# One of five products of the attention scores on half the rows of the array, for two query blocks side by side

## The chip, the cores and the metric

The kernel runs on one core of a Trainium2 chip. The metric is the time of one execution on the device in microseconds (us). Five engines work side by side on a core: TensorE (PE in the profile; its weight loads have a row of their own, PEld), VectorE (DVE), ScalarE (ACT), GpSimd (POOL) and SyncE (SP), which here only issues DMAs. TensorE multiplies a stationary operand, held in an array of 128 rows and 128 columns, with a moving operand that streams through it, and accumulates in the banks of PSUM. The rows of the array are the dimension that is summed over.

## The reference

One layer of a hybrid decoder over 1024 positions of width 1024: layer norm, one input projection, a state-space branch (S5) and an attention branch (MLA) beside each other, an output projection, a gated embedding, a closing layer norm. All is in 32-bit floats. What the change touches are the scores of the attention, with 4 heads and blocks of 128 queries:

```python
q = concatenate([q[..., :QK_NOPE], rotary(q[..., QK_NOPE:], cos, sin)], axis=-1)   # 128 + 64
k = concatenate([k_nope, broadcast(rotary(kr, cos, sin), heads)], axis=-1)
s = einsum('bqhd,bkhd->bhqk', qb, k) * scale
s = where(key_pos <= q_pos, s, -inf)
pr = softmax(s, axis=-1)
out = einsum('bhqk,bkhd->bqhd', pr, v)
```

The rotary part of a query has 64 numbers, that of a key too, and all heads share the keys' rotary part.

## The kernel before

**Split products.** TensorE takes its operands rounded to a shorter form. To stay near full precision, the kernel splits each operand into hi (the rounded value) and lo (the rest), and makes three products (`mm3`, line 518): hi by hi, hi by lo, lo by hi. Line 441, to which the profile puts every instruction, is only where the recorded instructions are issued; groups are told apart by their tiles.

**The scores** (`scores`, line 914) are made per head h and block qb of 128 queries, against the first n = (qb+1)*128 keys, in pieces c:e of at most 512 columns. A piece takes five products into one PSUM tile `s`. Three are an `mm3` of the part without rotation (tiles qnh, qnl, kh, kl). Two are of the rotary part. Since that has only 64 numbers, its tiles hold two copies one above the other: the 128 rows of `qr` are hi over lo of q, those of `krh` are twice the keys' hi, those of `krl` twice the keys' lo. So the product of `qr` with `krh` sums q hi and q lo by k hi in one go, and the product of `qr` with `krl` sums q hi and q lo by k lo:

```python
mm3(o, qn[h][0][:, q], qn[h][1][:, q], kh[:, c:e], kl[:, c:e], True, False)
mm(o, qr[h][:, q], L["kr"][0][:, c:e], False, False)
mm(o, qr[h][:, q], L["kr"][1][:, c:e], False, True)
```

The pieces are 128 columns (qb = 0), 256, 384, 512 (qb = 1 to 3), 320 and 320 (qb = 4), 512 and 256, 512 and 384, 512 and 512 (qb = 5 to 7). A score of up to 512 columns takes one of four small PSUM buffers (`PB`), a longer one takes one of two large ones (`PA`), which S5's tiles `w` and `y` use too. Then the softmax: VectorE adds the mask and takes the maximum (tile `p`, from `s`), ScalarE the exponential, and the result is scaled by the reciprocal of the sum.

**`q_rope`** (line 867) makes rotary q and splits it into the two halves of tile `qd`; `q_rope_t` transposes `qd` to `qr`.

**Items.** The attention goes through 16 items (h, j) in the order of the list `ATTEND`; an item is the two query blocks 2j and 2j+1. The loop at line 1522 writes, for each i: the scores of item i, the transposes of the probabilities of item i-1 (`probs_t`, tiles pt, pth, ptl), the product with the values of item i-2 (`pv`, tile o), the last projection of item i-3 (`uv_out`, tile uv), and late pieces of S5 and of its gate (`glu`).

**The order of the work.** The code doesn't issue instructions; it records them in a `Plan`. `Plan.issue` (line 308) then lays them out with prices of its own for each operation (for a product 0.012 us and 0.425 ns a column, at least 0.11 us where the weights change) and takes on each engine the ready instruction with the lowest number, once its buffers are free. So the order on each engine comes from the order of the recording, from the shifts in `AHEAD` and `SHIFT`, and from the prices. Whatever changes a price changes the order of all that comes after.

Of the kernel before, what the change touches and what calls it, by code (L numbers as in the profile page):

```python
# [17 lines left out]

# [1 line left out]

# [14 lines left out]
P = 128  # L35
# [84 lines left out]
class Plan:  # L120
# [74 lines left out]
    def record(self, ways, args=()):  # L195
        _, method, kw = ways[0]
        isap = lambda x: hasattr(x, "tensor") and hasattr(x, "ap")
        outs = [kw[k] for k in ("out", "accum_out") if isap(kw.get(k))]
        rest = [v for k, v in kw.items() if isap(v) and k not in ("out", "accum_out")]
        pos = [a for a in args if isap(a)]  # L200
        if "out" not in kw:
            outs.append(pos.pop(0))
        ins = rest + pos
        named = [v for k, v in kw.items() if k in ("in_", "in0", "in1", "data0", "data1") and isap(v)]
        tensors = named or pos[: 1 if method.startswith("tensor_scalar") else None]
        op = {
            "holds": {e for e, m, _ in ways if self.shares(e, m, outs[0], tensors)},
            "i": len(self.ops), "ways": {e: (m, self.cost(e, m, outs[0], ins, k), k) for e, m, k in ways},
            "args": args, "deps": set(self.behind), "tiles": set(), "pri": len(self.ops) + self.shift,
            "wait": self.URGENT if self.urgent else 0.0,  # L210
            "func": kw.get("func") if method == "activation" else None,
            "bytes": 4 * outs[0].size() if method == "dma_start" else 0,
            "stream": self.streams(outs[0]) if ways[0][0] == "T" else 0.0,
            "weights": (pos[0].tensor.name, pos[0].offset) if method == "matmul" else None,
        }
        for aps, w in ((ins, False), (outs, True)):
            for ap in aps:
                name = ap.tensor.name
                r = self.region(ap)
                seen = self.uses.setdefault(name, [])  # L220
                keep = []
                for j, q, qw in seen:
                    hit = r[0] < q[1] and q[0] < r[1] and r[2] < q[3] and q[2] < r[3]
                    if hit and (w or qw) and j != op["i"]:
                        op["deps"].add(j)
                    inside = r[0] <= q[0] and q[1] <= r[1] and r[2] <= q[2] and q[3] <= r[3]
                    if not (w and inside and j != op["i"]):
                        keep.append((j, q, qw))
                keep.append((op["i"], r, w))
                self.uses[name] = keep  # L230
                op["tiles"].add(name)
        self.ops.append(op)
# [75 lines left out]
    def issue(self):  # L308
        ops = self.ops
        n = len(ops)  # L310
# [37 lines left out]
                put(i)  # L348
        self.recent, self.cold = deque(), True
        hwdge = dma = ports = 0.0  # L350
        func = weights = None
        order = []
        plain = (None, AF.Copy, AF.Identity, AF.Square)

# [23 lines left out]
        while len(order) < n:  # L378
            best = None
            for e, lst in ready.items():  # L380
                can = []
                for i in lst:
                    s = start(i, e)
                    if s is not None:
                        late = e == "A" and ops[i]["func"] not in plain and ops[i]["func"] != func
                        can.append((s, ops[i]["pri"], i, 0.6 if late else 0.0))
                if not can:
                    continue
                soon = min(c[0] + c[3] for c in can)
                cand = min((c for c in can if c[0] + c[3] <= soon + ops[c[2]]["wait"]), key=lambda c: c[1])  # L390
                cand = (None, cand[0], cand[2])
                if cand and (best is None or cand[1] < best[0]):
                    best = (cand[1], cand[2], e)
            if best is None:
                raise RuntimeError("the written order does not fit the pools")
            s, i, e = best
            o = ops[i]
            for x in o["ways"]:
                ready[x].remove(i)
            ran[i] = e  # L400
            for t in o["tiles"]:
                if t in self.tag and t not in got:
                    got.add(t)
                    tag = self.tag[t]
                    waiting[tag].remove(t)
                    free[tag].pop(0)
            c = o["ways"][e][1]
            if e == "A" and o["func"] not in plain and o["func"] != func:
                func = o["func"]
                c += 1.28  # L410
            if e == "T":
                if o["weights"] is not None and o["weights"] != weights:
                    c = max(c, self.WEIGHTS)
                weights = o["weights"]
                c = self.clock(s, c, o["stream"])
            at[e] = s + c
            end = s + c
            if e in o["holds"]:
                ports = end
            if e == "S":  # L420
                hwdge = max(hwdge, s) + 0.46
                size = o["bytes"] / 358e3
                dma = max(dma, hwdge + 0.9) + size
                end = dma + 0.9
            done[i] = end
            order.append((s, len(order), i))
            for t in o["tiles"]:
                tile_end[t] = max(tile_end.get(t, 0.0), end)
                tile_left[t] -= 1
                if not tile_left[t] and t in self.tag:  # L430
                    free[self.tag[t]].append(tile_end[t] + 0.1)
            for u in users[i]:
                left[u] -= 1
                if not left[u]:
                    put(u)
# [9 lines left out]
def trunk(ctx, tc, I, out):  # L445
# [69 lines left out]
    def mm(ps, a, b, st, sp_):  # L515
        T.matmul(ps, a, b, start=st, stop=sp_)
# [350 lines left out]
    def q_rope(hf):  # L867
        qd = L["qd", hf] = [Hf("qd", F32R, (P, H, 2, 64)) for _ in range(4)]
        for j in range(4):
            t = hf * 4 + j  # L870
            ps = PB("qrp", (P, H, 64))
            for k in range(2):
                ch, cl = L["cq"][k]
                s = slice(t * P, t * P + P)
                mm3(ps, ch[:, s], cl[:, s], wqr[0][:, k], wqr[1][:, k], k == 0, k == 1)
            o = Hf("qro", shape=(P, H, 64))
            rotary(o, ps, *(x[:, t : t + 1].to_broadcast([P, H, 64]) for x in (cos, sin)))
            split(qd[j][:, :, 0], qd[j][:, :, 1], o)

    def q_rope_t(hf):  # L880
        qd = L.pop(("qd", hf))
# [29 lines left out]
    ym = {}  # L911
    gmr = {}

    def scores(h, qb):
        n = (qb + 1) * P
        q = slice(qb * P, qb * P + P)
        ps = PB("s") if n <= 512 else PA("s")
        kh, kl = L["k"]
        w = 512 if n % 512 != P else n // 2 if n > P else P
        for c in range(0, n, w):  # L920
            e = min(c + w, n)
            o = ps[:, c // w * 512 : c // w * 512 + e - c]
            mm3(o, qn[h][0][:, q], qn[h][1][:, q], kh[:, c:e], kl[:, c:e], True, False)
            mm(o, qr[h][:, q], L["kr"][0][:, c:e], False, False)
            mm(o, qr[h][:, q], L["kr"][1][:, c:e], False, True)
        p = U("p")
        mx = SM("mx", (P, 1), bufs=4)
        si, so, mk = ps[:, :n], p[:, :n], L["mask"][:, S - n :]
        if w < 512 and n > P:
            si = ps.rearrange("p (c n) -> p c n", c=2)[:, :, :w]  # L930
            so, mk = (x.rearrange("p (c n) -> p c n", c=2) for x in (so, mk))
        V.tensor_tensor_reduce(
            out=so, in0=si, in1=mk, scale=1.0, scalar=3.0 * MASK, op0=ALU.add, op1=ALU.max, accum_out=mx,
        )
        V.tensor_scalar_mul(mx, mx, -SCALE)
        sm = SM("rsum", (P, 1), bufs=4)
        act(p[:, :n], p[:, :n], AF.Exp, scale=SCALE, bias=mx, accum=sm)
        rc = SM("rrec", (P, 1), bufs=4)
        V.reciprocal(out=rc, in_=sm)
        plan.scaled("AVG", p[:, :n], p[:, :n], rc)  # L940
        return p
# [580 lines left out]
    for i in range(n + 3):  # L1522
        if i < n:
            h, j = items[i]
            pr[i] = [scores(h, 2 * j + q) for q in range(2)]
        k = i - 1
        if 0 <= k < n:
            pts[k] = probs_t(*items[k], pr.pop(k))
        k = i - 2
        if 0 <= k < n:  # L1530
            os[k] = pv(*items[k], pts.pop(k))
        k = i - 3
        if 0 <= k < n:
            uv_out(*items[k], os.pop(k))
        after(True)
# [91 lines left out]
```

## Time and profile before

| | |
|---|---|
| median of 3 runs | 593.2 us (592.72 to 593.23) |
| the profiled execution | 592.97 us |
| its span, from the first to the last instruction | 591.3 us |
| mean granted clock of TensorE | 0.992 |
| TensorE busy | 567.1 us, 3000 products |
| VectorE busy | 446.8 us |
| ScalarE busy | 281.6 us |
| scores, first to last start on TensorE | 262.3 to 364.0 us |

Three stretches make up the span: up to 262 us the norms, the projections and most of S5's preparation; from 262 to 365 us the attention, with S5's late pieces in between; after that the gate of S5, the output projection (tile op), the embedding's gate (tile g) and the closing norm. The stretches' busy time, with the columns stretch, length, TensorE, weight loads, VectorE, ScalarE, GpSimd (instructions in brackets), granted clock, DMA share and GB/s, is in such rows:

```profile
0.00:262.00 262.00, 250.46 (x1275) 209.97 (x1276) 232.63 (x513) 137.74 (x267) 40.98 (x51) 0.99 0.42 145
...
365.00:591.30 226.30, 215.43 (x1034) 180.20 (x1033) 125.07 (x198) 70.23 (x109) 10.98 (x14) 0.99 0.41 143
```

In a timeline a row has start, duration, engine, line, operation, result and operands, tile sizes and count; a bracket at its end tells how long the engine was idle before it, and what ended that. A product's duration runs to the end of its results, which lies after the start of the next product; the distance between starts tells what it costs.

### The profile page before, as it was taken

The numbers are of one execution on the slowest core, as the hardware profiler recorded it, in microseconds if no ns is written. First come the engines' busy times: TensorE is split into PE (matmuls) and PEld (weight loads), VectorE is DVE, ScalarE is ACT, GpSimd is POOL, SyncE is SP. The second block draws the span as 40 slices with busy tenths as digits, with TensorE's granted clock in tenths as the row PEclk, the third lists the DMA queues.
The fourth block names the chain that finished last, engine by engine and source line by source line (L and its number), as shares of the span: only waits on it lengthen the run. The fifth ranks groups of instructions, "written<-read, shape, count | busy, mean of one in ns | idle before, by whom it ended". The sixth has DMA issues, their size and how long they took to land.

```text
span 591.3 us, 8335 instructions
## 1 busy us (share of the span) xinstructions
PE 567.1 (96%) x3000; PEld 482.3 (82%) x3000; DVE 446.8 (76%) x952; ACT 281.6 (48%) x533; POOL 83.8 (14%) x100
## 2 busy tenths in 40 slices
PE   8989989999999999999999999899999999999994
PEld 6777868788898878878899998688888888888884
DVE  6999999989999986478989879876323226577666
ACT  5777136355383851367677786443222235133221
POOL 0000004201020234114522221010000010000000
PEclk9999989999999999999999999899999999999998
DMA  8897422532130512201013225326422438724301
GB/s 301 316 354 267 159 72 86 201 124 95 72 111 2 172 64 72 72 38 37 1 50 129 72 73 171 150 73 247 115 99 72 161 107 278 309 89 160 108 35 72
DMA packets 46233, 76.66 MB, mean 130 GB/s; under 512 B 4384, under 2 KB 27104, under 8 KB 46192
## 3 DMA queue, kind: packets, MB, share of 16 engines
q1 hardware_dynamic: 46192, 76.14, 37.3%
q8 instruction: 23, 0.38, 0.3%
q14 instruction: 18, 0.15, 0.1%
HBM read 50.47 MB, written 25.66 MB: 129 GB/s over the span
## 4 chain that ended last, share of the span: by engine, by line
PE 57%; DVE 4%; issue 1%; ACT 1%; DVEq 0%
PE op L441 15%; PE g L441 15%; PE s L441 6%; PE o L441 4%; PE z L441 4%; PE glu L441 3%; PE pt L441 2%; PE qn L441 2%; PE ut L441 1%; PE uv L441 1%; PE qrp L441 1%; DVE gsr L441 1%; PE y L441 1%; DVE p L441 1%; DVE hh L441 0%
## 5 line engine op out<-in xcount | busy, mean ns | idle before, releaser
L441 PE MATMUL z<-xh,wh 128*128 128x512 f32 x192 | 76.4, 398 | 1.2 <-DVE krh L441 1.2
L441 PE MATMUL z<-xh,wl 128*128 128x512 f32 x192 | 75.7, 396 | 1.1 <-DVE wl L441 1.1
L441 PE MATMUL z<-xl,wh 128*128 128x512 f32 x192 | 76.4, 398 | 0.0
L441 PE MATMUL g<-wph,uh 128*128 128x512 f32 (+1 forms) x136 | 51.4, 378 | 0.0
L441 PE MATMUL g<-wph,ul 128*128 128x512 f32 (+1 forms) x136 | 51.2, 377 | 0.0
L441 PE MATMUL g<-wpl,uh 128*128 128x512 f32 (+1 forms) x136 | 51.2, 377 | 0.0
L441 DVE SCALAR_TENSOR_TENSOR xr<-xr,op 128x512 f32<-128x512 f32 x16 | 11.0, 687 | 50.2 <-PE op L441 50.2
L441 PEld LDWEIGHTS z<-xh,wl 128*128 128x128 f32 x192 | 36.5, 190 | 8.6 <-DVE wl L441 1.7
L441 PEld LDWEIGHTS z<-xh,wh 128*128 128x128 f32 x192 | 36.5, 190 | 8.6 <-DVE krh L441 1.5
L441 PEld LDWEIGHTS z<-xl,wh 128*128 128x128 f32 x192 | 36.6, 190 | 6.9
L441 PEld LDWEIGHTS g<-wph,ul 128*128 128x128 f32 x136 | 25.6, 188 | 4.7
L441 PEld LDWEIGHTS g<-wpl,uh 128*128 128x128 f32 x136 | 25.6, 188 | 4.7
L441 PEld LDWEIGHTS g<-wph,uh 128*128 128x128 f32 x136 | 25.6, 188 | 4.6
L441 DVE CUSTOM_DVE_ANT_0 p<-s,mask 128x128 f32<-128x128 f32 (+7 forms) x32 | 23.8, 752 | 4.0 <-PE s L441 3.8
L441 ACT COPY ut<-ut 128x512 f32<-128x512 f32 x16 | 9.4, 588 | 35.3 <-PE ut L441 35.2
L441 PE MATMUL op<-ysh,woh 128*128 128x512 f32 x64 | 26.2, 409 | 0.0
L441 ACT ACTIVATE p<-p,mx 128x128 f32<-128x128 f32 (+7 forms) x32 | 24.8, 775 | 2.7 <-DVE mx L441 2.6
L441 DVE TENSOR_TENSOR ptl<-pt,pth 128x512 fp32r<-128x512 f32 (+3 forms) x48 | 25.3, 551 | 0.9 <-ACT pth L441 0.4
L441 ACT ACTIVATE sgg<-g 128x512 f32<-128x512 f32 (+1 forms) x17 | 9.6, 565 | 34.0 <-PE g L441 34.0
L441 PE MATMUL pt<-ident,p 128*128 128x128 f32 x144 | 21.5, 285 | 3.8 <-ACT sg L441 2.2
L441 PE MATMUL op<-ysh,wol 128*128 128x512 f32 x64 | 25.0, 391 | 0.0
L441 POOL TENSOR_TENSOR rstd<-ve,half 128x1 f32<-128x1 f32 (+1 forms) x10 | 7.1, 714 | 126.2 <-DVE ve L441 107.6
(370 smaller groups left out, 1673.1 us busy)
## 6 DMA issues: line engine op xcount, KB each, us to landing
wr<-in_w_fm SPq DMA_DIRECT2D x12, 512.0 KB, 5.6
x<-in_x SPq DMA_DIRECT2D x8, 512.0 KB, 8.7
d_pp<-ppo SPq DMA_DIRECT2D x8, 512.0 KB, 4.8
d_xln<-xt SPq DMA_DIRECT2D x16, 256.0 KB, 6.1
wor<-in_w_out SPq DMA_DIRECT2D x8, 512.0 KB, 5.8
xr<-d_xln SPq DMA_DIRECT2D x8, 512.0 KB, 5.2
d_ut<-ut SPq DMA_DIRECT2D x16, 256.0 KB, 2.4
utok<-d_ut SPq DMA_DIRECT2D x16, 256.0 KB, 4.2
```

Of the source, the lines that this page charges most:

```text
L441: getattr(self.real[ran[i]], method)(*ops[i]["args"], **kw)
```

## The change

The product with the keys' lo takes q's hi alone and 64 of the 128 rows: rows 0 to 63 for the even block of an item, rows 64 to 127 for the odd one. For that `q_rope` puts hi above lo for even blocks and lo above hi for odd ones; `krl` has the keys' lo in both halves already. The product of q's lo with the keys' lo is thereby left out of the sum. `scores` now records both blocks of an item together: all full products of the even block, all of the odd one, and then the products on 64 rows in turn, a piece of the even block and a piece of the odd one. After that come the two softmaxes (`soft`). The planner learns that a product on part of the rows, recorded after one on other rows that is still running by its reckoning, costs 0.02 us.

```diff
+            "rows": self.region(pos[0])[:2] if method == "matmul" and pos[0].shape[0] < P else None,
...
-                c = self.clock(s, c, o["stream"])
+                if o["rows"] and rows and o["rows"] != rows[0] and s < rows[1]:
+                    c, rows = self.clock(s, 0.02, 0.0), None
+                else:
+                    c = self.clock(s, c, o["stream"])
+                    rows = (o["rows"], s + c + 0.05) if o["rows"] else None
...
-            split(qd[j][:, :, 0], qd[j][:, :, 1], o)
+            hi = t % 2
+            split(qd[j][:, :, hi], qd[j][:, :, 1 - hi], o)
...
-    def scores(h, qb):
+    def scores(h, j):
+        kh, kl = L["k"]
+        todo, ps2 = ([], []), []
+        for i in range(2):
+            qb = 2 * j + i
+            n = (qb + 1) * P
+            q = slice(qb * P, qb * P + P)
+            ps = PB("s") if n <= 512 else PA("s")
+            ps2.append(ps)
+            w = 512 if n % 512 != P else n // 2 if n > P else P
+            r = slice(64 * i, 64 * i + 64)
+            for c in range(0, n, w):
+                e = min(c + w, n)
+                o = ps[:, c // w * 512 : c // w * 512 + e - c]
+                mm3(o, qn[h][0][:, q], qn[h][1][:, q], kh[:, c:e], kl[:, c:e], True, False)
+                mm(o, qr[h][:, q], L["kr"][0][:, c:e], False, False)
+                todo[i].append((o, qr[h][r, q], L["kr"][1][r, c:e]))
+        for x in zip_longest(*todo):
+            for v in x:
+                if v:
+                    mm(*v, False, True)
+        return [soft(h, 2 * j + i, ps2[i]) for i in range(2)]
+
+    def soft(h, qb, ps):
         n = (qb + 1) * P
-        q = slice(qb * P, qb * P + P)
-        ps = PB("s") if n <= 512 else PA("s")
-        kh, kl = L["k"]
         w = 512 if n % 512 != P else n // 2 if n > P else P
-        for c in range(0, n, w):
-            e = min(c + w, n)
-            o = ps[:, c // w * 512 : c // w * 512 + e - c]
-            mm3(o, qn[h][0][:, q], qn[h][1][:, q], kh[:, c:e], kl[:, c:e], True, False)
-            mm(o, qr[h][:, q], L["kr"][0][:, c:e], False, False)
-            mm(o, qr[h][:, q], L["kr"][1][:, c:e], False, True)
...
-            pr[i] = [scores(h, 2 * j + q) for q in range(2)]
+            pr[i] = scores(h, j)
```

More of the change, by code (lines that the diff above doesn't have):

```diff
@@ L17 @@
 from contextlib import ExitStack
+from itertools import zip_longest
 import numpy as np
@@ L350, in issue @@
         hwdge = dma = ports = 0.0
-        func = weights = None
+        func = weights = rows = None
         order = []
```

## The prediction

> **What bounds the kernel now.** I read the page's head first, then the busy time of the stretch that the change touches, then TensorE's waits.
>
> ```profile
> span 591.3 us, 8335 instructions
> PE 567.1 (96%) x3000; PEld 482.3 (82%) x3000; DVE 446.8 (76%) x952; ACT 281.6 (48%) x533; POOL 83.8 (14%) x100
> PE op L441 15%; PE g L441 15%; PE s L441 6%; PE o L441 4%; PE z L441 4%; PE glu L441 3%; PE pt L441 2%; PE qn L441 2%; PE ut L441 1%; PE uv L441 1%; PE qrp L441 1%; DVE gsr L441 1%; PE y L441 1%; DVE p L441 1%; DVE hh L441 0%
> ```
> ```profile
> 262.00:365.00 103.00, 101.20 (x695) 92.12 (x694) 89.07 (x242) 73.65 (x159) 31.84 (x36) 1.00 0.19 61
> ```
> ```profile
> PE pt L441 <- ACT sg L441: 2.2, 1, 2.2
> PE pt L441 <- DVE ol L441: 1.4, 2, 1.1
> ```
>
> TensorE is busy for 96% of the span. All products of the scores (tile s) lie between 262 and 365 us; there it is busy 101.2 of 103 us at a granted clock of 1.00, VectorE 89.1. So a column less on TensorE is time gained, except where the chain of waits runs through VectorE. VectorE is near enough to take over: of TensorE's waits the two largest are in this part.
>
> What a product costs is its distance to the next in the timeline of TensorE, not its length, since ends overlap. The columns are start, duration, engine, line, operation.
>
> ```profile
> 322.55 0.31 PE L441 MATMUL s<-kh,qnh 128*128 128x320 f32 x1
> ...
> 323.28 0.31 PE L441 MATMUL s<-kh,qnh 128*128 128x320 f32 x1
> ...
> 324.01 0.39 PE L441 MATMUL s<-kh,qnh 128*128 128x512 f32 x1
> ...
> 325.17 0.28 PE L441 MATMUL s<-kh,qnh 128*128 128x256 f32 x1
> ...
> 325.76 0.60 PE L441 MATMUL pt<-ident,p 128*128 128x128 f32 x4
> ...
> 331.06 1.37 PE L441 MATMUL pt<-ident,p 128*128 128x128 f32 x11
> 332.19 0.48 PE L441 MATMUL s<-kh,qnh 128*128 128x512 f32 x1
> 332.51 0.39 PE L441 MATMUL s<-kl,qnh 128*128 128x512 f32 x1
> ...
> 343.48 0.27 PE L441 MATMUL s<-kl,qnh 128*128 128x128 f32 x1
> ...
> 343.92 0.33 PE L441 MATMUL s<-kh,qnh 128*128 128x256 f32 x1
> ```
> ```profile
> 266.31 0.34 PE L441 MATMUL s<-kh,qnh 128*128 128x384 f32 x1
> ...
> 267.18 0.39 PE L441 MATMUL s<-kh,qnh 128*128 128x512 f32 x1
> 267.41 0.40 PE L441 MATMUL s<-kl,qnh 128*128 128x512 f32 x1
> ```
>
> Five products of a piece of keys stand between its first row and the next piece's. So a product takes (323.28-322.55)/5 = 0.146 us at 320 columns, (325.17-324.01)/5 = 0.232 at 512, (325.76-325.17)/5 = 0.118 at 256, (267.18-266.31)/5 = 0.174 at 384, and (343.92-343.48)/4 = 0.110 at 128. The last is not half of 0.118: there the weight loads rule, which follow one another at the same distance:
>
> ```profile
> 263.39 0.19 PEld L441 LDWEIGHTS s<-krh,qr 128*128 128x128 f32 x1
> 263.50 0.19 PEld L441 LDWEIGHTS s<-krl,qr 128*128 128x128 f32 x1
> 263.61 0.19 PEld L441 LDWEIGHTS s<-kh,qnl 128*128 128x128 f32 x1
> ...
> 267.19 0.19 PEld L441 LDWEIGHTS s<-kl,qnh 128*128 128x128 f32 x1
> 267.42 0.19 PEld L441 LDWEIGHTS s<-kh,qnl 128*128 128x128 f32 x1
> ```
>
> At 512 columns a load begins with the product before its own (267.19 beside 267.18) and is hidden behind it.
>
> **The change, part by part.** *The pairs.* A head has four items j = 0 to 3. The lo products of the two query blocks of an item become pairs of 64 rows: j = 0 pairs 128 with 256 columns, j = 1 384 with 512, j = 2 320 with 512 and 320 with 256, j = 3 512 with 512 and 384 with 512. That is 6 pairs a head, 24 in all, from these 48 products:
>
> ```profile
> L441 PE MATMUL s<-krl,qr x48: 273/335/481, 263.6 to 364.0; 128*128 128x512 f32 x20, 128*128 128x256 f32 x8, 128*128 128x384 f32 x8, 128*128 128x320 f32 x8
> ```
>
> If the halves of the array work side by side, a pair takes as long as its longer member, yet no less than its two weight loads, 2 x 0.110 = 0.22 us. Saved are: j = 0, 0.110+0.118-0.22 = 0.008; j = 1, 0.174; j = 2, 0.146 and 0.146+0.118-0.22 = 0.044; j = 3, 0.232 and 0.174. That makes 0.778 a head, 3.11 us for four. No row of this trace has a product on 64 rows (all 3000 are 128*128), so this is the upper end. The next end is that the second load isn't hidden behind the product before the pair but begins with the pair's first product; the second then starts 0.11 late, and a pair takes the longer of its first member and 0.11 plus its second: 0, 0.064, 0.036, 0.036, 0.122 and 0.064 saved, 0.322 a head, 1.3 us. The lowest end is no overlap at all: 0. I take 3.1, since the product ahead of the pair is mostly 0.23 us long and two loads of 0.11 fit behind it.
>
> The Trainium skill ("TensorE: Matmul & The Clock Gate", Part 3) says that products in different row groups start about 4 ns apart, which speaks for the same end; no run here shows it.
>
> *The switch of the array.* Each of the 16 items goes from 128 rows to 64 and back, 32 switches, and the trace has none. The nearest row is the step from transposes to products: 332.19 to 332.51 is 0.32 us where 0.232 is the rule, 0.09 more, a load that a short predecessor doesn't hide. Pairs of 0.23 us hide it; those of j = 0 don't, 4 x 0.09 = 0.36 us. Lower bound 0; upper bound that the array runs empty at each switch. A product of 512 columns is shown as 398 ns long where the next comes after 232, so 0.166 us are what is under way when the next begins:
>
> ```profile
> L441 PE MATMUL s<-krl,qr 128*128 128x512 f32 x20 | 8.0, 398 | 0.0
> ```
>
> That would be 32 x 0.166 = 5.3 us. I take 0.36, from the row for a change of kind that the trace does have.
>
> By the Trainium skill ("TensorEngine Tiling (Array Packing)", Key Properties), a change of the tiling mode, not merely of the tile, drains the TensorE. By that rule the sum would be the first rival's below; no run here shows it, and this speaks against the change.
>
> *Where the gain is lost.* The chain of waits leaves TensorE twice in the scores' stretch:
>
> ```profile
> 276.53 0.69 DVE p L441
> ...
> 280.68 0.63 PE pt L441 x4
> ...
> 290.67 0.42 DVE p L441
> ...
> 296.01 0.86 PE o L441 x5
> ```
>
> ```profile
> 277.39 0.40 PE L441 MATMUL s<-krl,qr 128*128 128x512 f32 x1
> ...
> 279.77 0.28 PE L441 MATMUL s<-krl,qr 128*128 128x256 f32 x1
> ```
> ```profile
> 292.14 0.40 PE L441 MATMUL s<-krl,qr 128*128 128x512 f32 x1
> ...
> 292.91 0.33 PE L441 MATMUL s<-krl,qr 128*128 128x384 f32 x1
> ...
> 294.01 0.39 PE L441 MATMUL s<-krl,qr 128*128 128x512 f32 x1
> ...
> 295.16 0.39 PE L441 MATMUL s<-krl,qr 128*128 128x512 f32 x1
> ```
>
> Between those times TensorE waits for VectorE in the end, and what it saves there is given back. In the second stretch lie the four lo products of one item with j = 3 (0.232+0.174 = 0.41 us of the gain), in the first the second block's of one with j = 2 (0.146+0.044 = 0.19); another order could bring some of it back. I take 0.5 us (0 to 0.8).
>
> *The later first softmax.* Both blocks of an item now end with the pairs, so the first block's maximum on VectorE starts later by the second block's eight other products: for j = 3, 8 x 0.232 = 1.9 us, less for the others. In the middle of the stretch other items' transposes and value products cover it, because the transposes of an item come only after the next item's scores. At the end nothing follows:
>
> ```profile
> 361.03 1.09 DVE L441 CUSTOM_DVE_ANT_0 p<-s,mask 128x896 f32<-128x896 f32 x1
> ...
> 364.38 1.23 DVE L441 CUSTOM_DVE_ANT_0 p<-s,mask 128x1024 f32<-128x1024 f32 x1 [0.54 <-PE s L441]
> ```
>
> The 1.09 us operation would fall just ahead of the 1.23 us one, on the chain. VectorE's idle 0.54 us and the gate work that waits (yTh, gsr) can change places with it. Bounds 0 and 1.1; I take 0.3. If TensorE had no other work here, it would be the whole 1.1.
>
> *At nothing.* The split of rotary q writes hi into the other half for odd blocks: the same ACT and POOL operations on the same shapes, and the same transposes after them. The left-out product, q's lo by the keys' lo, saves no instruction. No DMA moves and no queue but TensorE's gets another order by hand. The planner does: it prices a pair's second product at 0.02 us and lays every engine's order after 262 us anew. What it hides above, it may also unhide; I give that +-0.8 us and put it into the range only.
>
> **Sum.** 3.1 - 0.36 - 0.5 - 0.3 = 1.9 us faster. The profiled execution took 592.97 us (span 591.3 and 1.7 around it), so 591.1 for it; the median of the three runs is 593.2, 0.2 above, hence 591.3.
>
> **Rivals.** *The array empties at each switch* (slower). Place: the first of the pair after the keys' hi product, and the first full product after the pair. Price: 32 times what is under way, up to 0.166 us each. It decides from (3.1-0.5-0.3)/32 = 0.07 us a switch; at the full 0.166 the sum is 5.3-2.3 = 3.0 us slower, 596.2, at half that 0.4, 593.6. If the weights' load waits too (0.11 more, at both ends of 16 groups, 3.5 us) it would be 599.7. For it: the two halves end in different rows and all 128 rows must be free again. Against: transposes and products alternate in the trace with 0.09 us at most. By the Trainium skill's rule cited above, this is what happens.
>
> *Side by side only in part, or not at all*: the second load waits for the first product, or the halves take turns. Gain 1.3 less 0.36, 0.2 of the 0.5, and 0.3: 592.8; or none, with 0.36 and 0.3 lost: 593.9. No change that can be told. For it: loads here begin one product ahead and never two (267.19 and 267.42). The planner may also put another product between the members of a pair.
>
> *The held buffers.* A score of over 512 columns holds one of two large PSUM buffers, and now both until VectorE has read the first block 1.1 us after the pairs. Where two neighbouring items have j of 2 or 3, the next item's scores start that much later unless 1.1 us of other work is ready: 2 such places in the list of items, 2.2 us, more than the gain of 1.9: 593.5; the S5 tiles of the same buffers could add to it. Against: the 11 transposes from 331.06 to 332.19 last as long as that read.
>
> **How the numbers follow.** A change of 0.2%, 1.2 us, is about what a measurement of this kernel can tell from none. Forecast 0.50, drain 0.26, partial overlap 0.17, buffers 0.07. The forecast's own bounds are 590.1 (3.1 us and nothing lost) to 592.4 (0.36, 0.8 and 1.1 lost): 0.44 of it is faster by over 0.2%, 0.06 within. Drain: 0.22 slower, 0.04 within. Partial: 0.04 faster, 0.11 within, 0.02 slower. Buffers: 0.05 within, 0.02 slower. So faster 0.48, same 0.26, slower 0.26. The range reaches down to the full 3.1 us with a favourable order (589.5) and up to most of the drain case (595.8), past which about 0.1 is left.
>
> **What would show it.** Right: lo products of 64 rows with starts some 0.01 to 0.11 us apart and two loads in a row ahead of them; the first full product after a pair no later than 0.23 to 0.32 us; tile s busy less by about 3 us; the maxima of one item adjacent on VectorE. Wrong: gaps of 0.1 us and more on either side of each pair (drain); starts of a pair as far apart as its first is long (no overlap); TensorE's wait on VectorE's p between neighbouring items (buffers); TensorE's busy time less by 3 us and the span unchanged (VectorE the bound).

## The result, and the profile after

The changed kernel takes 609.76 us (median of 4 runs, 609.36 to 610.18), the kernel before beside it 592.96 us (592.72 to 593.23). The ratio is 1.0277, with an interval of 1.0262 to 1.0291: 16.8 us slower. The prediction was 591.3 with a range up to 595.8. It was wrong in its sign, and the range doesn't hold the result. One of the nine runs of kernel e14 below took 936 us at a granted clock of 0.56, and its median leaves that run out.

The head of the page of after, its busy time and its chain by line:

```profile
span 607.4 us, 8353 instructions
PE 571.5 (94%) x3000; PEld 481.1 (79%) x3000; DVE 449.2 (74%) x955; ACT 278.4 (46%) x529; POOL 84.0 (14%) x101
PE op L447 14%; PE g L447 14%; PE s L447 6%; PE z L447 4%; PE o L447 4%; PE glu L447 4%; PE pt L447 2%; PE qn L447 2%; PE ut L447 1%; DVE gsr L447 1%; PE qrp L447 1%; PE uv L447 1%; DVE p L447 0%; PE y L447 0%; PE qrt L447 0%
```

The span grew by 16.1 us, TensorE's busy time by 4.4. So some 12 us are not work but waiting. The stretches of the windows view say where (columns as in the table of before):

```profile
0.00:262.00 262.00, 250.69 (x1275) 210.02 (x1276) 232.56 (x513) 137.39 (x267) 40.99 (x52) 0.99 0.42 145
262.00:365.00 103.00, 91.53 (x607) 79.08 (x605) 76.83 (x210) 63.70 (x138) 23.97 (x28) 0.97 0.15 48
```

Up to 262 us nothing changed. In the scores' stretch TensorE was busy 101.2 us of 103 before and is busy 91.5 now, and it gets through 607 products there instead of 695. The largest of TensorE's waits are new; engine, tile, whom it waited for, then us in total, times, longest:

```profile
PE pt L447 <- POOL p L447: 8.1, 2, 7.8
PE glu L447 <- DVE yTl L447: 4.6, 1, 4.6
```

The first two are single stalls, of 7.8 and of 4.6 us. The first one on TensorE and on GpSimd, which it waits for:

```profile
283.06 0.55 PE L447 MATMUL pt<-ident,p 128*128 128x128 f32 x3
291.42 1.11 PE L447 MATMUL pt<-ident,p 128*128 128x128 f32 x4 [7.81 <-POOL p L447]
```
```profile
290.67 0.69 POOL L447 TENSOR_SCALAR p<-p,rrec 128x512 f32<-128x512 f32 x1 [10.28 <-DVE rrec L447]
```

GpSimd isn't slow here; it waits 10.3 us for `rrec`, a reciprocal of 0.16 us on VectorE. ScalarE had the sum for it ready at 280.9 us (its row starts at 280.70 and takes 0.19). VectorE's timeline shows what stood ahead:

```profile
280.30 0.67 DVE L447 TENSOR_TENSOR rt<-im,ec 128x512 f32<-128x512 f32 x1
280.88 0.69 DVE L447 TENSOR_TENSOR rt<-rt,rt 128x512 f32<-128x512 f32 x1
...
283.01 2.31 DVE L447 TENSOR_TENSOR_SCAN rt<-mg,rt 128x128 f32<-128x128 f32 x7
...
287.62 2.76 DVE L447 TENSOR_TENSOR hh<-rt,rt 64x508 f32<-64x508 f32 x4
290.41 0.16 DVE L447 RECIPROCAL rrec<-rsum 128x1 f32<-128x1 f32 x1
```

From 280.30 to 290.38 VectorE works without a gap on the last block of S5, and the softmax queues behind it. In the kernel before, GpSimd did the six operations ahead of the scans, 1.3 us each, and VectorE had room for the softmax ahead of the scans and between them. GpSimd's timeline of before:

```profile
275.94 1.29 POOL L441 TENSOR_TENSOR rt<-re,ec 128x512 f32<-128x512 f32 x1 [4.48 <-DVE re L441]
...
282.43 1.31 POOL L441 TENSOR_TENSOR rt<-rt,re 128x512 f32<-128x512 f32 x1
```

In after GpSimd does two of the six and VectorE four. Of the four operations between the scans and `hh`, GpSimd did three in before and does none in after. These operations may run on either engine (`VG`), and the planner puts each where its own reckoning ends it sooner. With the scores in another order that reckoning came out differently; which of its prices tipped it, no run shows.

The second stall lies at the end of the attention. VectorE's timeline of after, then that of before:

```profile
384.10 4.48 DVE L447 TENSOR_TENSOR gsr<-gsr,yT 128x1024 f32<-128x1024 f32 x2
388.52 1.21 DVE L447 TENSOR_TENSOR yTl<-yT,yTh 128x1024 fp32r<-128x1024 f32 x1
```
```profile
368.80 1.23 DVE L441 TENSOR_TENSOR yTl<-yT,yTh 128x1024 fp32r<-128x1024 f32 x1
369.94 3.78 DVE L441 TENSOR_TENSOR gsr<-gsr,yT 128x1024 f32<-128x1024 f32 x2
```

The same two operations in the other order: 4.48 us that nobody needs yet (gsr) now stand ahead of 1.21 us that TensorE's glu waits for. The hi half of this split, yTh, has moved too: VectorE made it at 368.09 us in before, ScalarE makes it at 382.78 in after, for 1.03 us.

The products on 64 rows themselves are all there, 48 of them, in the forms that the change asks for:

```profile
L447 PE MATMUL s<-krl,qr x48: 276/403/500, 264.0 to 377.9; 64*128 64x512 f32 x20, 64*128 64x256 f32 x8, 64*128 64x384 f32 x8, 64*128 64x320 f32 x8
```

In the trace the first two products of a group, one on each half, start 2 to 5 ns apart. One pair does not stay together: the planner put full products between the two members of an item with j = 0 (starts 301.46 and 302.62), so after goes to 64 rows and back 17 times, not 16. What that costs is read from the distances. TensorE's timeline of after around a group with j = 3 (rows of 64*128 are grouped, x4), then the weight loads in the same place:

```profile
310.37 0.40 PE L447 MATMUL s<-krh,qr 128*128 128x512 f32 x1
310.69 0.74 PE L447 MATMUL s<-krl,qr 64*128 64x512 f32 x4
311.36 0.55 PE L447 MATMUL pt<-ident,p 128*128 128x128 f32 x3
```
```profile
310.14 0.19 PEld L447 LDWEIGHTS s<-krh,qr 128*128 128x128 f32 x1
310.69 0.30 PEld L447 LDWEIGHTS s<-krl,qr 64*128 64x128 f32 x4 [0.36 <-issue]
311.36 0.31 PEld L447 LDWEIGHTS pt<-ident,p 128*128 128x128 f32 x3 [0.37 <-issue]
```

A load of full rows begins with the product before its own (310.14 is 0.23 ahead of 310.37). The load for 64 rows doesn't: it begins at 310.69, 0.32 us after the last full product, which has a slot of 0.232. So 0.09 us pass between the end of that slot and the load, which I read as the array running empty, and then a load of 0.11 is in the open. On the way back it is the same. From the end of the full product's slot (310.37+0.232 = 310.60) to the time at which the next full products go on as usual (311.36+0.11 = 311.47) is 0.87 us. The two pairs need 2 x 0.232 = 0.46 of it, the two changes of rows 0.41. The four products took 3 x 0.232 + 0.174 = 0.87 before: nothing is won with j = 3, the best case. With one pair (j = 1) it is a loss:

```profile
325.10 0.40 PE L447 MATMUL s<-krh,qr 128*128 128x512 f32 x1
325.43 0.49 PE L447 MATMUL s<-krl,qr 64*128 64x384 f32 x2
325.85 0.55 PE L447 MATMUL pt<-ident,p 128*128 128x128 f32 x3
```

325.85+0.11-(325.10+0.232) = 0.63 us, against 0.232+0.174 = 0.41 before. In the same way j = 2 takes 0.75 against 0.64 and j = 0 takes 0.51 against 0.23. A head loses 0+0.11+0.22+0.28 = 0.61 us, the four heads 2.4. The broken pair loses 0.35 and 0.40 us in place of 0.28, so the rows of after give 2.9.

### The profile page after: what moved, and what is told of

Read it like the earlier page. It is cut to its first block, busy times and chain, and to the rows that moved or that the text cites. A ratio compares the mean times of both kernels' runs of the same rounds, so it can differ in the third digit from the quotient of the medians.

```text
span 607.4 us, 8353 instructions
## 1 busy us (share of the span) xinstructions
PE 571.5 (94%) x3000; PEld 481.1 (79%) x3000; DVE 449.2 (74%) x955; ACT 278.4 (46%) x529; POOL 84.0 (14%) x101
## 4 chain that ended last, share of the span: by engine, by line
PE 55%; DVE 4%; issue 3%; ACT 1%; POOL 0%; DVEq 0%; POOLq 0%
PE op L447 14%; PE g L447 14%; PE s L447 6%; PE z L447 4%; PE o L447 4%; PE glu L447 4%; PE pt L447 2%; PE qn L447 2%; PE ut L447 1%; DVE gsr L447 1%; PE qrp L447 1%; PE uv L447 1%; DVE p L447 0%; PE y L447 0%; PE qrt L447 0%
## 5 line engine op out<-in xcount | busy, mean ns | idle before, releaser
L447 PEld LDWEIGHTS pt<-ident,p 128*128 128x128 f32 x144 | 16.5, 145 | 14.1 <-POOL p L447 8.7
```

The costliest lines, as they stand in the source:

```text
L447: getattr(self.real[ran[i]], method)(*ops[i]["args"], **kw)
```

## The experiments

The experiments are to tell three things apart: (a) the array's change of rows, about 0.40 us a group, (b) the six S5 operations, (c) a price of the later softmax, which I first held to be covered by other work, and of VectorE's order at the end. Rivals: that the change of rows is the whole loss, or that the later softmax is. All ratios are to the kernel before, measured again beside each group of kernels; its medians were 594.17, 593.58, 593.19, 593.28 and 593.76 us. Where a kernel makes the lo product on 64 rows of q's hi (e2, e3, e6, e8, e12, e5, e13), q's lo by the keys' lo is left out, as in the changed kernel. The others have the whole sum.

**Before's order, one part of the change at a time.** e3 starts from the kernel before's order on all engines, takes an item's lo products out of it and puts them, as pairs, where the odd block's last one stood. What then isn't ready is passed by what is, so the order doesn't stay quite the same: by the traces of e3, e4 and e6, three of VectorE's 32 maxima, two `ol`, a `yTl`, a few reciprocals and two operations of ScalarE have changed places with others, and on TensorE three products of a score have gone ahead of eight S5 products (tile w). e4 moves them in the same way and leaves them on 128 rows. e6 puts both members of a pair on rows 0 to 63, so that they can't run side by side. The diff is e3's, which has the change's split of rotary q too; `paired` does the moving. In e4 the product stays as it was, in e6 `r` is `slice(0, 64)` and the split as before.

```diff
-            for _, _, i in sorted(order):
+            for i in self.paired([i for _, _, i in sorted(order)]):
...
-            mm(o, qr[h][:, q], L["kr"][1][:, c:e], False, True)
+            r = slice(qb % 2 * 64, qb % 2 * 64 + 64)
+            mm(o, qr[h][r, q], L["kr"][1][r, c:e], False, True)
+            plan.lo.setdefault((h, qb), []).append(len(plan.ops) - 1)
```

> The order of before on every engine; only the lo products of an item are moved, as a group of pairs on 64 rows, to where the odd block's last one stood. Theory (each change of the array between 128 and 64 rows costs about 0.2 us, read from after's starts, and after's order of the other work costs the rest): 16 groups lose 32 x 0.2 = 6.4 us and gain 3.9 by running side by side, so 2.5 slower than before, plus whatever the later softmax costs: 595.0 to 597.5. Rival A (the 64-row products themselves make up all 16.8 us of after's loss): 605 to 610. Rival B (the array gains what I predicted, and only the order of the other work is bad): 589.5 to 591.5.

> The same order as the pairs in before's order, instruction by instruction, but the lo products take all 128 rows, as in before. What differs from before is only that the even block's lo products, and so its softmax, come later. Theory: 593.0 to 594.5, since other work covers a later softmax in this order. Rival (the later softmax or the PSUM buffers held longer make the loss): 597 or more.

> The same order again, the lo products on 64 rows, but both members of a pair on rows 0 to 63, so that they cannot run side by side. Theory: 3.9 us more than the pairs on two halves, 599 to 601, which is the gain of side by side by itself. Rival (the halves do not overlap, or the weight loads rule): the same time as the pairs on two halves, within 0.7.

Measured: e3 606.06 us, 1.0205 [1.0178, 1.0232]; e4 604.82, 1.0187 [1.016, 1.0214]; e6 608.29, 1.0244 [1.0217, 1.0271]. My expectations for e3, e4 and e6 fell: with every product on full rows and the six S5 operations on GpSimd, ending the even block's sums later costs 10.7 us. This is the price of the later softmax with all that it holds up; e4 doesn't part it from the few changed places, nor from the large PSUM buffers held longer (S5's products w, which use them, wait 1.2 us for `mx` and 0.8 us for `im` in its trace, and in before not at all). Waits of e4 from 255 to 390 us, VectorE's and ScalarE's, then the same rows of before (255 to 375):

```profile
DVE p L482 <- PE s L482: 7.9, 11, 2.1
...
ACT p L482 <- DVE mx L482: 13.8, 11, 3.3
```
```profile
DVE p L441 <- PE s L441: 3.8, 7, 1.0
...
ACT p L441 <- DVE mx L441: 2.9, 6, 1.1
```

Each engine works through its instructions in a set order: in e3, e4 and e6 it is the same on every engine, at different times. When the scores come up to 1.9 us later, VectorE stands longer at the maximum, then ScalarE at the exponential. No stall is large (none on TensorE over 2.5 us), but they add up from item to item.

That the halves do run side by side shows in the rows of e3 and e6 around a pair of 384 and 512 columns:

```profile
322.79 0.49 PE L482 MATMUL s<-krl,qr 64*128 64x384 f32 x2
323.21 0.98 PE L482 MATMUL pt<-ident,p 128*128 128x128 f32 x7
```
```profile
323.00 0.67 PE L482 MATMUL s<-krl,qr 64*128 64x384 f32 x2
323.60 0.98 PE L482 MATMUL pt<-ident,p 128*128 128x128 f32 x7
```

0.42 us in e3, 0.60 in e6: the 0.18 between them is what a product of 384 columns takes. On the whole time e6 is 2.2 us over e3, with intervals that overlap.

**e2: before's order untouched, each lo product by itself on rows 0 to 63.**

```diff
-            mm(o, qr[h][:, q], L["kr"][1][:, c:e], False, True)
+            mm(o, qr[h][0:64, q], L["kr"][1][0:64, c:e], False, True)
```

> Exactly before's order on every engine; each lo product takes rows 0 to 63 alone, where it stood. 48 times from 128 rows to 64 and back, no pairs. Theory: 48 x 0.4 = 19 us slower, 607 to 613, less what lies in stretches that wait for VectorE. Rival B (a change of rows costs nothing): 593 to 594.

Measured: 608.42 us, 1.0252 [1.0221, 1.0283], so 14.3 us more, as expected. Here nothing moved; only the array changes its rows at each of 48 products:

```profile
331.65 0.40 PE L441 MATMUL s<-krh,qr 128*128 128x512 f32 x1
331.98 0.49 PE L441 MATMUL s<-krl,qr 64*128 64x512 f32 x1
332.40 0.38 PE L441 MATMUL s<-kh,qnh 128*128 128x256 f32 x1
332.62 0.28 PE L441 MATMUL s<-kl,qnh 128*128 128x256 f32 x1
```

Distances of 0.33, 0.42 and 0.22 us where 0.232, 0.232 and 0.118 are the rule: 0.39 us for going in and out once, at 48 places 18.7 us, of which 14.3 reach the end. The change of rows is a cost by itself, without any reordering.

**e1, e5, e7: the planner's new order, and the six S5 operations.** e1 has after's order on every engine with the lo products on 128 rows. e5 is the changed kernel with the six operations held on GpSimd for the last block; e7 is the kernel before with them held on VectorE (`V` in place of `Gp`). The diffs of e1 and e5:

```diff
-            "rows": self.region(pos[0])[:2] if method == "matmul" and pos[0].shape[0] < P else None,
+            "rows": self.half,
...
-                todo[i].append((o, qr[h][r, q], L["kr"][1][r, c:e]))
+                todo[i].append((o, qr[h][:, q], L["kr"][1][:, c:e], r))
...
-                    mm(*v, False, True)
+                    plan.half = (v[3].start, v[3].stop)
+                    mm(*v[:3], False, True)
+                    plan.half = None
```

```diff
+        vg = Gp if b == 3 else VG
-        mul(a, re, c, VG)
+        mul(a, re, c, vg)
...
-        sub(e, e, re, VG)
+        sub(e, e, re, vg)
```

> After's order on every engine, instruction by instruction, but the lo products take all 128 rows, so q's lo by the keys' lo is back in the sum. Theory: only the array's own loss of 2.5 us goes away, so 606.5 to 609; the order alone makes some 14 us. Rival A (the 64-row products make the loss): 592 to 595. Rival B (the array gains 3 us and the order loses 20): 612 to 613.5.

> After, but the six operations ahead of the scans of S5's last block (b = 3) are given to GpSimd, where before had them; the planner lays out the rest. Theory: after's order is bad because VectorE takes four of them and with them ten us of S5 without a gap, while a reciprocal and the transposes of a softmax wait behind; so most of the 14 us of the order come back: 596 to 600. Rival A: no change from after, 608 to 611. Rival C (the long wait only moves to another place): 604 to 608.

> Before with no change to the scores, but the same six operations of S5's last block given to VectorE; the planner lays out the rest. Theory: before gets most of after's loss without any product on 64 rows: 602 to 609. Rival C (it is no more than where such a chain falls, and here it falls on nothing): 593 to 597.

Measured: e1 607.68 us, 1.0233 [1.0206, 1.0259]; e5 599.09, 1.0094 [1.0072, 1.0116]; e7 605.75, 1.0205 [1.0172, 1.0238]. All three as expected. Most of the loss is in the order and not on the array (e1), 10.7 us of it hang on those six operations in the changed kernel (e5), and moving them costs the kernel before 12.2 us (e7), through the same stall, now of 10.6 us (the row below). In e5 and e7 the planner, which lays out the rest, lets some of the four operations behind the scans go along: GpSimd does two of them in e5 and none in e7.

```profile
PE pt L441 <- POOL p L441: 11.5, 2, 10.6
```

**e8, e9, e12: the pairs first.** The pairs are recorded ahead of an item's full products and open the sums, so the even block's softmax can start right after its own products. e9 has e8's order on 128 rows; e12 has it with both members on rows 0 to 63.

```diff
-                mm3(o, qn[h][0][:, q], qn[h][1][:, q], kh[:, c:e], kl[:, c:e], True, False)
-                mm(o, qr[h][:, q], L["kr"][0][:, c:e], False, False)
                 todo[i].append((o, qr[h][r, q], L["kr"][1][r, c:e]))
+                full[i].append((o, q, slice(c, e)))
         for x in zip_longest(*todo):
             for v in x:
                 if v:
-                    mm(*v, False, True)
-        return [soft(h, 2 * j + i, ps2[i]) for i in range(2)]
+                    mm(*v, True, False)
+        out = []
+        for i in range(2):
+            for o, q, c in full[i]:
+                mm3(o, qn[h][0][:, q], qn[h][1][:, q], kh[:, c], kl[:, c], False, False)
+                mm(o, qr[h][:, q], L["kr"][0][:, c], False, True)
+            out.append(soft(h, 2 * j + i, ps2[i]))
+        return out
```

> The same pairs on 64 rows as after, with the same price to the planner, but recorded ahead of an item's full products instead of behind them: the pairs open the sums in PSUM, the even block's last product is a full one, and its softmax is recorded right after it. Theory (the even block's late softmax makes some 12 us of after's loss, the change of the array's rows some 2.5): the late softmax is gone, the array's loss stays, 594.5 to 597.5. Rival B (any new layout by the planner loses about ten us, wherever the pairs stand): 602 to 612. Rival A (the array makes the loss): 605 or more.

> The order of the pairs ahead, instruction by instruction on every engine, but the lo products take all 128 rows. Theory: 2.5 us less than with the pairs ahead, so 592 to 595, the time of before, though the planner laid everything out anew. Rival B: 600 or more.

> The order with the pairs first (1.010 of before), both members of every pair on rows 0 to 63, so that nothing can run side by side; q's lo is left out of this product as in the changed kernel. If the overlap saves the 3.9 us that the rows give (the shorter member of each of 24 pairs): 602.3 to 603.5, a ratio to before of 1.0155 to 1.0175. Rival: the halves don't gain on the whole, because what one half saves is lost in the wait for weights: 599 to 600.5, 1.010 to 1.0125.

Measured: e8 599.01 us, 1.010 [1.008, 1.012]; e9 594.97, 1.0035 [1.002, 1.0049]; e12 601.0, 1.014 [1.0119, 1.016]. In this order the six operations stay on GpSimd. e9 is as expected, e8 1.5 us over what I gave it; the two stand 4.0 us apart, the price of the array with an equal order. But this order isn't one of 16 groups. The planner tore 11 of the 24 pairs apart; TensorE's timeline of e8 around an item with j = 0:

```profile
289.55 0.28 PE L447 MATMUL uv<-oh,wuvl 128*128 128x256 f32 x1
289.76 0.32 PE L447 MATMUL s<-krl,qr 64*128 64x128 f32 x1
290.01 0.33 PE L447 MATMUL s<-kh,qnh 128*128 128x128 f32 x1
```

The product of the even block stands alone, and that of the odd one, of 256 columns, starts at 292.75. In all, e8 goes to 64 rows and back 24 times at about 0.40 us, and 13 pairs run side by side: by the rows it loses 7.3 us, where 16 whole groups would lose 2.4. That is more than enough for the 1.5 us. e12 lies between the two expectations and loses 9.5 us by the rows. So being side by side is worth 2.2 us in this order by the rows, and the medians of e8 and e12 show 2.0.

**e10: e4 with only the four items of j = 3 moved** (`if qb == 6` in place of `if qb % 2 == 0`).

> Before's order with all 128 rows; only in the four items with j = 3 the even block's two lo products, and with them its softmax, come after the odd block's. In the run with all sixteen items late 10.6 us went for a delay of 4 x (0.47 + 0.93 + 1.4 + 1.9) = 18.8 us in all, 0.57 us for each. Theory: in proportion, 4 x 1.9 x 0.57 = 4.3 us slower than before, 3 to 6. Rival (the loss comes from single places in the order, not from the delay): 0 to 1, or more than 8.

Measured: 598.59 us, 1.0088 [1.0072, 1.0104], 5.4 us more, within the expectation: a part of the delay brings a part of the loss. By its trace one maximum, of 896 columns, some small operations and the eight S5 products have changed places here.

**e11, e13, e14: both places of VectorE's order put right.** e11 is e1 with the six operations on GpSimd. e13 is e5, e14 is e11, both with the split of the last yT ahead of the gate's products, and with its hi half held on VectorE, as before had it:

```diff
-        split(h, l, y)
+        split(h, l, y, V if k == 3 else AV)
+        if k == 3:
+            Y["end"] = (len(plan.ops) - 1,)
...
+        plan.behind = Y.get("end", ())
         mul(g, g, Y[m][0].rearrange("p (j n) -> p n j", j=CT))
+        plan.behind = ()
```

> The changed kernel's order with the six S5 operations of the last block on GpSimd, and the lo products on all 128 rows. The same on 64 rows stood at 1.0094 of before. If the change of the array's rows costs what the rows of the trace say (0.40 us for each of 16 groups against 3.9 us of overlap, 2.4 us net) up to what the pair with equal order said (4.0 us): 595.0 to 596.7 beside 593.2 of before, a ratio of 1.003 to 1.006. Rival: the array costs nothing in this order, and the rest of the loss is the later softmax alone: 598.5 to 599.5, 1.009 to 1.0105.

> The changed kernel with the six S5 operations of the last block on GpSimd (1.0094 of before by itself) and, at the end of the attention, with the gate's two products (gsr by yT, 4.5 us on VectorE) behind the split of the last yT instead of ahead of it. The traces of the changed kernel, and of its full-row twin, show TensorE 4.6 us idle there, and the twin goes from 0.9 us ahead of before to 3.0 us behind at that place. If that order is what the rest of the loss is: 594.5 to 596.5 beside 593.2 of before, 1.0025 to 1.0055, and what is left is the array's change of rows. Rival: the wait only moves on to the gate's later use (tile sg), since VectorE has the same work: 598 to 599.5, 1.008 to 1.0105.

> The same order on every engine with the lo products on all 128 rows. If the two places of VectorE's order are the whole of the loss beside the array: 592.0 to 594.0, a ratio of 0.998 to 1.0015, so that the softmax recorded after the other block's products costs nothing by itself. Rival: the later softmax has a price of its own that the planner can't lay out: 595.5 to 597.5, 1.004 to 1.0075. The distance to the kernel on 64 rows is the array: 2 to 4 us.

Measured: e11 597.23 us, 1.0065 [1.0048, 1.0082], half a microsecond over the first expectation; e13 595.97, 1.0043 [1.0029, 1.0057], as expected; e14 595.02, 1.0023 [1.0011, 1.0035], between the first expectation and the rival's. e13 and e14 are 1.0 us apart, less than the 2 to 4 us that I expected of the array. The wait of glu on yTl is down to 0.2 us in e13 and e14, and the medians are lower by 3.1 us (e5 to e13) and 2.2 us (e11 to e14). The way from after back to before is thereby, in ratios: 1.0277, less the six operations 1.0094, less the gate's order 1.0043, less the array's change of rows 1.0023, and 1.4 us that stay.

One product late in the attention, the thirteenth one from `ol` by `wuv` into uv, shows the array's part ahead of the gate's stall. TensorE's timelines of e5 and e11:

```profile
370.55 0.28 PE L447 MATMUL uv<-ol,wuv 128*128 128x256 f32 x1
```
```profile
368.36 0.28 PE L448 MATMUL uv<-ol,wuv 128*128 128x256 f32 x1
```

e5, on 64 rows, is 2.2 us behind e11, which has the same order. The rows of e5, with 17 changes there and back, give 3.1 for the whole attention. Against before e11 is 0.9 us ahead here (369.25 in before), but that says little, since the two orders differ: at the twelfth such product it is 1.5 us behind (363.10 against 361.63).

## Why the prediction was wrong

**A column less is time gained: true only while the order holds.** I read TensorE's 101.2 busy us of 103 as a bound, and named VectorE as the one that could take over. It did, but not by being full: at two places the work of VectorE was laid out otherwise. The reading of the waits beside it was wrong too: the wait of 2.2 us ends at 373.05 us, behind the scores' stretch, in which the longest is 1.1.

**"The planner does": +-0.8 us, the step that failed most.** The prediction saw that the planner lays every engine's order after 262 us anew and gave that 0.8 us, a number taken from no row. It measured 10.7 us for the S5 operations (after to e5) and 3.1 for the gate (e5 to e13), 13.8 of 16.8 us (10.9 and 3.0 by the ratios, since these kernels weren't measured beside each other). The six operations on GpSimd stood in the trace of before (275.94 to 283.74 us), and the code says that they may go to either engine. Such a placement should have been a rival with a stall of its own.

**The pairs, 3.1 us: right in kind.** The halves do work side by side (starts 2 to 5 ns apart, and 0.42 against 0.60 us for a pair). By the rows that is 3.8 us if all 24 pairs stay together. The medians show 2.2 us (e3 to e6) and, with 13 pairs together, 2.0 us (e8 to e12), both with intervals that overlap.

**The switch, taken at 0.36 us: too small by a factor of 17.** It is 0.37 to 0.41 us a group, 16 x 0.39 = 6.2 us. The choice fell on the row of a step from transposes to products, which has all 128 rows on both sides and says nothing of a change of rows. The first rival had the mechanism, and its prices, 0.166 us a switch without the load and 0.276 with it, enclose the measured 0.20: 0.09 us until the load begins, and the load in the open for 0.11. By the Trainium skill ("TensorEngine Tiling (Array Packing)", Key Properties) a change of the tiling mode drains TensorE; the trace agrees, with 0.09 us before the load and 0.20 in all each time. I had given this case 0.26. With 6.2 for the switch the prediction's own sum is 3.1-6.2-0.5-0.3 = 3.9 us slower, 597.1, the right sign but past the range, and still far from 609.8. The whole times of two kernels with equal order give the array as 2.1 (after to e1; 2.6 by the ratios), 1.2 (e3 to e4), 4.0 (e8 to e9, with 24 changes there and back), 1.9 (e5 to e11) and 1.0 us (e13 to e14). The medians are a loss in all five; the intervals lie apart in the first and third alone. The 0.5 us for stretches in which TensorE waits was not measured by itself; in e2, 14.3 of the 18.7 us of the rows reached the end.

**The later first softmax, 0.3 us: it depends on who lays the order.** That other items' work covers it holds when the order is laid out for it: e14 loses 1.4 us in all. It doesn't hold when the order was made for the earlier scores: e4 loses 10.7. At the end of the attention the 1.09 us maximum did fall just ahead of the 1.23 us one in after (378.26 and 379.27 us), within the bound of 1.1. I also wrote that the gate work "can change places with it". What changed places were two pieces of the gate work itself, gsr and the split of yT, and that cost 3.1.

**The other rivals.** "Side by side only in part, or not at all" is excluded by the starts and by the rows of e3 and e6 for pairs that stay together; but the planner did put other products between the members of a pair, as that rival had it, once in after and 11 times in e8. "The held buffers" showed only a little: in after, scores wait 0.9 us for the softmax and 1.4 us, in two waits, for S5's `im`, the read that frees a large buffer; before has no such wait.

**Still open.** The last 1.4 us of e14 aren't put down to anything. What share of the array's loss by the rows reaches the end varies with the order: 14.3 of 18.7 us in e2, 4.0 of 7.3 in e8, 1.9 of 3.1 in e5, 1.0 of 3.1 in e13; why isn't settled. Why the planner moved the S5 operations, and gsr ahead of yTl, isn't followed through its prices. None of the fourteen kernels beats the kernel before.

## What to carry to other kernels

Products on part of the array's rows pay only if a group of them saves more than the way in and out costs, here 0.40 us, so gather many pairs or leave them, and see in the trace that they stay together. If they end a sum, all that waits for the sum is delayed; if they open it, that delay is gone, but here the planner then tore the pairs apart. If a list scheduler lays out your engines' order, a change of one term moves choices that lie far from it: look in the trace of before for the operations that may run on either engine and for long operations that may pass a short, awaited one, and give such a flip its own price. When the time goes up by much more than the busy time, look first for the one or two long waits, and hold the old placement there before you judge the change itself.

## What the hardware showed that I had not expected

**The clock after a stall.** The 7.8 us stall costs more than its length, since the granted clock falls. The windows view of after for the 4 us behind it, and TensorE's timeline in them:

```profile
291.40:295.40 4.00, 3.98 (x16) 3.76 (x17) 4.00 (x12) 1.80 (x4) 2.65 (x3) 0.52 0.00 0
```
```profile
293.18 0.42 PE L447 MATMUL o<-ptl,vh 128*128 128x256 f32 x1
293.39 0.41 PE L447 MATMUL o<-pth,vl 128*128 128x256 f32 x1
...
295.41 0.39 PE L447 MATMUL qn<-cqh,wf 128*128 128x512 f32 x1
295.64 0.40 PE L447 MATMUL qn<-cql,wf 128*128 128x512 f32 x1
```

At a granted clock of 0.52 a product of 256 columns takes 0.21 us instead of 0.118; from 295.41 on 512 columns take 0.23 again. Four us at about half speed are some 2 us more, which by this estimate brings the stall to 9.8 of the 10.7 that e5 gets back. The stall of 4.6 us is followed by 4 us at 0.50 too (389.7 to 393.7), but of the 6.6 us that the same estimate gives only 3.1 came back in e13, where TensorE waits 1.3 and 1.1 us at other places. The Trainium skill ("TensorE: Matmul & The Clock Gate", Part 1) has the clock at half after an idle window of about 3.4 us until TensorE was busy for about as long; the trace is near that, with about 4.0 us at half after idle times of 7.8 and of 4.6.

**Loads and a change of rows.** Loads of 128 rows run one product ahead. Across a change between 128 and 64 rows they don't, in either direction (0.36 and 0.37 us without a load around the group of j = 3).
